# First queries and keys computed side by side as x arrives, the next weights loaded ahead of the other query and key weights, and the last store issued from ScalarE's queue

## The chip, the cores and the metric

The kernel runs on one core of a Trainium2 chip. The metric is the device time of one execution in microseconds (us). The profile names the engines PE (TensorE, the matmuls), PEld (TensorE's weight loads), DVE (VectorE), ACT (ScalarE), POOL (GpSimd) and SP (SyncE, which issues most DMAs). SPq and ACTq are the instruction queues of SP and ScalarE, where their DMAs are issued.

## The reference

One layer of a decoder for 512 prompt tokens and 8 x 4 sample tokens (544 columns together, d_model 1024), all in fp32:

```
glu_a, glu_b, q, k, v, g_conv, g_att = split(x @ w_in)
u = glu_a * sigmoid(glu_b)
conv_out = silu(layer_norm(causal_depthwise_conv(u, 31 taps))) @ w_conv_proj
o = stick_breaking_attention(q, [past_k, k], [past_v, v])   # samples: 4096 past tokens by pages
mixed = (sigmoid(g_conv)*conv_out + sigmoid(g_att)*(o @ w_att_proj)) @ w_out
x = layer_norm(2**0.25 * x + mixed)
x = layer_norm(2**0.25 * x + (silu(gate) * up) @ w_ffn_down + sigmoid(x @ w_ple_gate) * (p @ w_ple))
```

The past keys and values of the samples are 256 pages each, found by a page table. The outputs are the new x, k, v and the last GLU rows.

## The kernel before, in words

**Products.** Everything lies transposed, channels on the partitions and the 544 tokens in the columns. An fp32 matrix is split into a high part (fp32r) and a low part (the rest); a product of one 128 x 128 weight tile with one x chunk is three passes, high x high, high x low and low x high (`passes`, `products`). `products(p, cols, nk, rhs, base, ks)` adds up `nk` chunks in one PSUM tile; `gemm` takes a PSUM tile `g` (2 x 512 columns, two buffers) and does all eight. For queries and keys only the 512 prompt columns are computed this way (`PROMPT`).

**Weights.** `W` is a row of units of 128 x 1024 fp32 (512 KB, eight 128 x 128 tiles) in the order of use. `ORDER` begins with units q0, k0, b0, a0, v0 (units 0 to 4), then q1, k1 and so on; b and a are the two halves of the GLU. `w_load` issues a unit's load from SP, `w_split` splits one half of it (512 columns) with `split`: the high part goes to ScalarE (or VectorE), the low part, wl, to VectorE or GpSimd. Split halves live in four buffers each (`wh`, `wl`). `FIRST` is the list of the eight query and key units, 0, 1, 5, 6, 10, 11, 15 and 16. They lie in slots of their own (`wq`); other units come through three buffers `wr`.

**Sample projection.** The samples' 32 columns are projected apart: `first_sample` waits for all of x, and then `project` multiplies x, not split, with all eight query and key units (z<-wq,xr, 128 matmuls), in two halves: the queries' four units, then the keys'. Its result goes through two transposes to `qblk` and `ks`, and `decode` begins. `scores` and `decode` run over K/V pages, which `prefetch` loads from SP into at most 17 slots `kv`; the slots come free when the scores and the weighted sums are done.

**Order.** The program is written out by a planner, `Weave`. `main` is a generator that writes the large matmuls; side streams (loads, splits, prompt attention, convolution, decode) have a priority and are stepped whenever their condition holds by the planner's own clocks: `wv.t` for TensorE, `act`, `dve`, `pool`, and `dma` with 0.357 MB a microsecond. `wv.ready` keeps for each tile, by name, the time at which it is ready by those clocks. So the order of each engine's instructions is fixed when the program is built, and a change in the first instructions can shift the order of all that follow. On the chip the engines then wait for one another by semaphores.

**The start.** `main` writes ten warming matmuls, then issues from SP the eight x chunks (272 KB each), with the two halves of unit 0 behind x chunks 0 and 1 (the first half from ScalarE's queue), then the constants `cvt`, `cct` and the page table `ptt`. The other seven units of `FIRST` follow. The side stream `start` splits each x chunk at the time at which the planner expects it; after chunk 1 it starts `loader` (units 2, 3, 4 into `wr`, and later ones as buffers come free) and `splitter` (unit 1 on). The queries of unit 0 and the keys of unit 1 are two gemms, one after the other, each evacuated by ScalarE into `qk`.

**The end.** The last norm's second half is finished by `last`: four tiles of two chunks each; VectorE multiplies, ScalarE applies gain and bias (for chunk 7, VectorE does), and SP stores the output rows: chunks 0, 1, 6 and 7 each by its own DMA, the others in pairs (`give`).

Of the kernel before, what the change touches and what calls it, by code (L numbers as in the profile page):

```python
# [12 lines left out]
AF = mybir.ActivationFunctionType  # L13
# [7 lines left out]
NT = 544  # L21
HT = 272
# [11 lines left out]
BASE, NU = {}, 0  # L34
# [141 lines left out]
def step_kernel(ctx: ExitStack, tc: tile.TileContext, xT, pT, ck, cvv, state, pt, W, cv, cc, yT, kT, vT, cvo):  # L176
    nc = tc.nc
# [21 lines left out]
    def slot(name, shape=(128, 2, NT), dt=F32):  # L199
        return big.tile(list(shape), dt, tag="s", bufs=NSLOT, name=name)  # L200
# [26 lines left out]
    def load(eng, out, in_):  # L227
        eng.dma_start(out=out, in_=in_)  # L228
        moved(out)
        wv.ready[out.name] = wv.dma + 1.5  # L230
# [140 lines left out]

    def loader():
        for u in range(NU):
            if u in FIRST:
                continue
            if u in AGAIN:
                yield lambda: AGAIN[u] in kept
                raw[u] = kept.pop(AGAIN[u])
                continue
            if u in SLOTTED:  # L380
                yield lambda: u * 8 <= cur["pos"] + 8 * WAHEAD
            elif u in PAIR and u == PAIRS[PAIR[u]][1]:
                yield lambda: u * 8 <= cur["pos"] + 40 and cur["wp"] < 3
            else:
                yield lambda: u * 8 <= cur["pos"] + 32 and cur["raw"] < 3
            w_load(u)

    def splitter():
        for u in range(1, NU):
            if u in PAIR:  # L390
                if u == min(PAIRS[PAIR[u]]):
                    yield lambda: u * 8 <= cur["pos"] + 15
                    yield from pair_splits(PAIR[u])
                continue
            yield lambda: u in raw and u * 8 <= cur["pos"] + 15
            yield on(raw[u])
            for e in range(2):
                if held(u) == "w":
                    yield lambda: cur["w"] < 4
                w_split(u, e)  # L400
# [229 lines left out]
    qk = []  # L630
# [438 lines left out]
    def first_sample(xr, wq):  # L1069
        yield on(*xr)  # L1070
        o = []
        yield from project(8, lambda k: xr[k // 2][:, k % 2, 512:544],
                           lambda c, k: wq[ORDER.index(("qk"[c // 4], c % 4))][:, k * 128:(k + 1) * 128], o)
        xr.clear()
        wq.clear()
        tp = o.pop()
        for m in range(4):
            for hh in range(2):
                r = slice(64 * hh, 64 * hh + 64)
                V.tensor_scalar(out=qblk[r, :, m, (2 * m + hh) * 4:(2 * m + hh) * 4 + 4],  # L1080
                                in0=tp[r, m * 32:(m + 1) * 32].rearrange("p (s q) -> p s q", q=4),
                                scalar1=0.125, scalar2=None, op0=ALU.mult)
        V.tensor_copy(out=ks.rearrange("p m q -> p (m q)"), in_=tp[:, 128:256])
        flag.add("qs")
        wv.add(decode(), 1)
# [18 lines left out]
    def main():  # L1104
# [4 lines left out]
            T.matmul(warm[:, :128], lhsT=on_m, rhs=on_m, start=True, stop=True)  # L1109
        del warm  # L1110
        xr = [slot("xr") for g in range(4)]
        raw[0] = slot("wq", (128, 1024))
        come = {}
        for c in range(8):
            load(nc.sync, xr[c // 2][:, c % 2], xT[c // 2][:, c % 2 * NT:(c % 2 + 1) * NT])
            come[c] = wv.dma + 1.5
            if c < 2:
                h = slice(512 * c, 512 * c + 512)
                load(nc.scalar if c == 0 else nc.sync, raw[0][:, h], W[0][:, h])
                come["w", c] = wv.dma + 1.5  # L1120
            if c == 7:
                load(nc.sync, cvt, cv)
                load(nc.sync, cct, cc)
                load(nc.sync, ptt, pt)
        for u in FIRST[1:]:
            w_load(u)
        nc.gpsimd.memset(qblk, 0.0)
        nc.gpsimd.memset(anew, 0.0)
        nc.gpsimd.memset(eps, EPS)
        wv.add(first_sample(list(xr), dict(raw)), 2)  # L1130
        wv.add(prefetch(), 0)
        wv.add(sample_tail(), 4)
        x_tiles.extend((slot("xh", dt=F32R), slot("xl", dt=F32R)) for g in range(4))

        def start():
            for c in range(8):
                yield At(come[c])
                h, lo = (t[:, c % 2] for t in x_tiles[c // 2])
                x_hl.append((h, lo))
                split(h, lo, xr[c // 2][:, c % 2])  # L1140
                if c < 2:
                    yield At(come["w", c])
                    w_split(0, c)
                if c == 1:
                    wv.add(loader(), -1)
                    wv.add(splitter(), -1)
            xr.clear()
        wv.add(start(), -1)

# [16 lines left out]
        vs = v2 = None  # L1166
        wv.add(prompt_attention(), 2)
        wv.add(conv(), 3)
        for w, m in ORDER:
            o = []  # L1170
            if w in "qk":
                yield from gemm(xin, 8, o, PROMPT)
            else:
                yield from gemm(xin, 8, o)
            p = o.pop()
            if w == "q":
                qk.append(slot("qk"))
                S.activation(out=qk[m][:, 0, 0:512], in_=p[:, 0], func=AF.Copy, scale=0.125)
            elif w == "k":
                S.activation(out=qk[m][:, 1, 0:512], in_=p[:, 0], func=AF.Copy)  # L1180
                flag.add(("k", m))

                def keys(m=m, t=qk[m]):
                    yield done("qs")
                    V.tensor_copy(out=t[:, 1, 512:544], in_=ks[:, m])
                    yield on(t)
                    store(kT[m], t[:, 1])
                wv.add(keys(), 0)
            elif w == "b":
                u = slot("u", (128, 814))  # L1190
                us[m] = u
                nc.gpsimd.memset(u[:, 0:30], 0.0)
                load(nc.sync, u[:, 542:814], state[m])
                yield spare(2)
                sg = tmp("sg")
                sigmoid(sg, p[:, :, :HT], sg, halves(sg), ("sg", m))
            elif w == "a":
                wv.add(glu(m, us[m], p, sg), 0)
                sg = None
            else:  # L1200
                yield spare(1)
                vt = tmp("vt")
                S.activation(out=halves(vt), in_=p[:, :, :HT], func=AF.Copy)
                wv.when(on(vt), lambda m=m, vt=vt: store(vT[m], vt))
                if m % 2 == 0:
                    v2 = slot("v", (128, 2, 512))
                if m == 0:
                    vs = slot("vs", (128, 2, 512))

                def back(m=m, vt=vt, v2=v2):  # L1210
                    yield wv.bank("tp")
                    tp = bank("tp")
                    for kt in range(4):
                        tr(tp[:, kt * 128:(kt + 1) * 128], vt[:, kt * 128:kt * 128 + 128])
                    V.tensor_copy(out=v2[:, m % 2], in_=tp)
                    v_sb[m] = v2[:, m % 2]

                    def sample():
                        yield wv.bank("tp")
                        tp = bank("tp")  # L1220
                        for r in range(2):
                            tr(tp[:, r * 128:(r + 1) * 128], vt[:, 400 + 16 * r:528 + 16 * r])
                        V.tensor_copy(out=vs[:, :, m * 128:(m + 1) * 128],
                                      in_=tp[:, :256].rearrange("p (r c) -> p r c", r=2))
                        drop()
                        if m == 3:
                            v_sb["vs", 0], v_sb["vs", 1] = vs[:, 0], vs[:, 1]
                    wv.when(on(v2), sample)
                wv.when(on(vt), back)
# [389 lines left out]
        def last(i, p):  # L1619
# [41 lines left out]
            for g in range(4):  # L1661
                if g > 1:
                    centred(g)
                V.tensor_tensor(out=xs[g], in0=xs[g], in1=r.to_broadcast([128, 2, HT]), op=ALU.mult)
                yield on(xs[g])
                for i in range(2 * g, 2 * g + 2):
                    if i == 7:
                        V.tensor_scalar(out=xs[g][:, 1], in0=xs[g][:, 1], scalar1=cvt[:, L2G + i:L2G + i + 1],
                                        scalar2=cvt[:, L2B + i:L2B + i + 1], op0=ALU.mult, op1=ALU.add)
                    else:  # L1670
                        S.activation(out=xs[g][:, i % 2], in_=xs[g][:, i % 2], func=AF.Identity,
                                     scale=cvt[:, L2G + i:L2G + i + 1], bias=cvt[:, L2B + i:L2B + i + 1])
                    if g in (0, 3):
                        nc.sync.dma_start(out=yT[i][:, HT:], in_=xs[g][:, i % 2])
                if g in (1, 2):
                    give(g, HT)

# [130 lines left out]
```

## Time and profile before

| | |
|---|---|
| time of three runs | 993.13 us median, 991.53 to 996.7 |
| time of the profiled execution | 992.45 us |
| span of its profile, first to last instruction | 990.6 us |
| mean granted TensorE clock | 0.986 |
| busy: PE, PEld, DVE, ACT, POOL | 950.3, 831.2, 781.3, 539.2, 163.2 us |
| moved by DMA | 222 MB, 224 GB/s over the span |

The time of an execution holds 1.85 us more than the span. In the page's 40 slices a digit is the busy share of a slice of 24.8 us in tenths. In the timeline each row is: start, duration, engine, line, operation, output<-inputs, shape and count, and in brackets the idle time of the engine before it and what ended that. Line L146 stands for all operations of VectorE, ScalarE and GpSimd (they go through one helper), L238 for all matmuls, L228 for all loads, L1674 and L1578 for stores of the output.

### The profile page before, as it was taken

The page shows a single profiled execution, that of the slowest core. Times are in us where ns is not written, and L with a number is a line of the kernel's source. Part 1 is how long each engine was busy: PE and PEld are TensorE (multiplying, and loading weights), DVE is VectorE, ACT ScalarE, POOL GpSimd, SP SyncE. Part 2 cuts the span into 40 slices and gives each one's busy share as a digit, 9 for nine tenths or more (in the row PEclk, how much of TensorE's full clock was granted, in tenths as well). Part 3 has the DMA queues.
Part 4 walks back from the last instruction along what each step waited for, and adds up shares of the span by engine and source line. Part 5 has one row for each costly group of instructions (what it writes and reads, how often), then busy time and mean ns, then how long its engine had stood idle before and what let it go on. Part 6 is the DMA issues. An engine that isn't in the chain of part 4 may idle for free.

```text
span 990.6 us, 22509 instructions
## 1 busy us (share of the span) xinstructions
PE 950.3 (96%) x8026; PEld 831.2 (84%) x8026; DVE 781.3 (79%) x1288; ACT 539.2 (54%) x1042; POOL 163.2 (16%) x147
## 2 busy tenths in 40 slices
PE   9989999999899999999999889999999999999995
PEld 7866566667677887788878789999999999999994
DVE  3798798999964666466698687999999999943366
ACT  4634766575786785244467564544554555622224
POOL 1230313223211102033343110000000000220020
PEclk9999899999999999999999899999999999999998
DMA  9948989999989999999999635223223221322302
GB/s 356 339 160 298 336 301 330 313 324 328 311 281 339 311 346 330 342 367 351 325 335 352 250 108 193 86 88 126 86 91 123 86 95 56 100 93 87 128 1 90
DMA packets 101393, 222.00 MB, mean 224 GB/s; under 512 B 11169, under 2 KB 14498, under 8 KB 101282
## 3 DMA queue, kind: packets, MB, share of 16 engines
q1 hardware_dynamic: 99410, 217.46, 62.5%
q10 hardware_dynamic: 1872, 3.11, 0.8%
q8 instruction: 63, 1.03, 0.4%
q14 instruction: 48, 0.39, 0.1%
HBM read 215.45 MB, written 5.07 MB: 223 GB/s over the span
## 4 chain that ended last, share of the span: by engine, by line
PE 74%; DVE 10%; DMA 9%; SPq 3%; issue 2%; ACT 2%; POOL 0%; ACTq 0%; DVEq 0%; POOLq 0%
PE g L238 44%; PE z L238 10%; PE av L238 9%; PE o L238 5%; PE tp L238 5%; DVE c L146 3%; DMA kv<-in_cvv 2%; SPq L228 2%; DMA kv<-in_ck 2%; DVE pb L146 2%; DMA wr<-in_W 2%; PE tp L243 1%; DMA xr<-in_xT 1%; SPq L657 1%; DMA wa<-in_W 1%
## 5 line engine op out<-in xcount | busy, mean ns | idle before, releaser
L146 ACT ACTIVATE wh<-wr 128x512 fp32r<-128x512 f32 x236 | 146.9, 628 | 201.1 <-PE g L238 99.8
L146 DVE TENSOR_TENSOR wl<-wr,wh 128x512 fp32r<-128x512 f32 x196 | 135.1, 694 | 52.1 <-ACT wh L146 50.8
L146 POOL TENSOR_TENSOR wl<-wr,wh 128x512 fp32r<-128x512 f32 x44 | 70.2, 1598 | 493.0 <-DVE pw L146 259.8
L238 PE MATMUL g<-xh,wh 128*128 128x272 f32 (+1 forms) x512 | 127.6, 320 | 0.3 <-ACT wh L146 0.3
L238 PE MATMUL g<-h,wh 128*128 128x272 f32 x704 | 122.2, 290 | 0.0
L238 PE MATMUL g<-xl,wh 128*128 128x272 f32 (+1 forms) x512 | 119.3, 304 | 0.8 <-DVE xl L146 0.8
L238 PE MATMUL g<-xh,wl 128*128 128x272 f32 (+1 forms) x512 | 118.8, 303 | 0.2 <-POOL wl L146 0.2
L146 DVE SCALAR_TENSOR_TENSOR c<-u,cvt,c 128x512 f32<-128x512 f32 x120 | 111.6, 930 | 3.3
L238 PEld LDWEIGHTS g<-h,wh 128*128 128x128 f32 x704 | 103.2, 189 | 0.3
L238 PEld LDWEIGHTS g<-xh,wh 128*128 128x128 f32 x512 | 82.9, 191 | 22.2 <-issue 17.5
L238 PEld LDWEIGHTS g<-xl,wh 128*128 128x128 f32 x512 | 83.7, 191 | 3.6 <-DVE xl L146 1.5
L238 PEld LDWEIGHTS g<-xh,wl 128*128 128x128 f32 x512 | 83.1, 191 | 4.0 <-POOL wl L146 0.9
L238 PE MATMUL g<-h,wl 128*128 128x272 f32 x352 | 80.1, 289 | 0.0
L146 ACT ACTIVATE wh<-wq 128x512 fp32r<-128x512 f32 x87 | 54.5, 628 | 40.5 <-PE g L238 29.5
L238 PE MATMUL z<-kv,qblk 128*32 128x256 f32 x1024 | 64.6, 381 | 1.1 <-DMA kv<-in_ck 1.1
L238 PE MATMUL g<-x1h,wh 128*128 128x272 f32 (+2 forms) x216 | 64.0, 296 | 0.0
L238 PE MATMUL av<-kv,dp 128*32 128x512 f32 x512 | 63.8, 612 | 0.0
L146 DVE TENSOR_TENSOR wl<-wq,wh 128x512 fp32r<-128x512 f32 x75 | 54.6, 733 | 11.4 <-ACT wh L146 11.0
L238 PE MATMUL g<-x1l,wh 128*128 128x272 f32 (+2 forms) x216 | 62.6, 290 | 0.0
L238 PE MATMUL g<-x1h,wl 128*128 128x272 f32 (+2 forms) x216 | 62.6, 290 | 0.0
L146 ACT ACTIVATE pa<-pa 128x384 f32<-128x384 f32 (+1 forms) x96 | 52.5, 555 | 17.2 <-DVE pa L146 15.6
L238 PEld LDWEIGHTS g<-h,wl 128*128 128x128 f32 x352 | 58.0, 188 | 0.0
(315 smaller groups left out, 2352.8 us busy)
## 6 DMA issues: line engine op xcount, KB each, us to landing
kv<-in_ck SPq DMA_DIRECT2D x256, 256.0 KB, 4.4
kv<-in_cvv SPq DMA_DIRECT2D x256, 256.0 KB, 5.4
wr<-in_W SPq DMA_DIRECT2D x98, 512.0 KB, 4.2
wq<-in_W SPq DMA_DIRECT2D x37, 512.0 KB, 5.1
wa<-in_W SPq DMA_DIRECT2D x12, 512.0 KB, 10.2
xr<-in_xT SPq DMA_DIRECT2D x8, 272.0 KB, 5.6
out_yT<-pw SPq DMA_DIRECT2D x6, 272.0 KB, 2.3
out_kT<-qk ACTq DMA_DIRECT2D x4, 272.0 KB, 6.1
```

The costliest lines, as they stand in the source:

```text
L146: fn(**kw)
L228: eng.dma_start(out=out, in_=in_)
L238: T.matmul(out, lhsT=lhsT, rhs=rhs, start=start, stop=stop)
L243: T.transpose(out, in_, ident)
L657: reg[col] = nc.sync.value_load(ptt[0:1, col:col + 1], min_val=0, max_val=POOL - 1)
```

## The change

- Both units 0 and 1 get their slots at once, and the first loads go in one list: x chunk 0, first half of unit 0, x 1, x 2, first half of unit 1, x 3, second half of unit 0, x 4, x 5, second half of unit 1, x 6, x 7. `start` splits them in this order.
- Behind the constants, units 2 and 3 are loaded ahead of the other six units of `FIRST`. `loader` begins with unit 4, `splitter` with unit 2, and both are started after the last x chunk is split.
- The first queries and the first keys share one PSUM tile (columns of its two halves). Their products alternate: query chunk k, then key chunk k - 2. Both are evacuated behind the last key product.
- The store of chunk 7 at the end is issued from ScalarE's queue.

```
-            if u in FIRST:                                   # loader
+            if u in FIRST or u < 4:
-        for u in range(1, NU):                               # splitter
+        for u in range(2, NU):
...
-        raw[0] = slot("wq", (128, 1024))
+        for u in range(2):
+            raw[u] = slot("wq", (128, 1024))
         come = {}
+        first = (0, ("w", 0, 0), 1, 2, ("w", 1, 0), 3, ("w", 0, 1), 4, 5, ("w", 1, 1), 6, 7)
+        for i, c in enumerate(first):
+            if c in range(8):
+                load(nc.sync, xr[c // 2][:, c % 2], xT[c // 2][:, c % 2 * NT:(c % 2 + 1) * NT])
+            else:
+                h = slice(512 * c[2], 512 * c[2] + 512)
+                load(nc.scalar if i == 1 else nc.sync, raw[c[1]][:, h], W[c[1]][:, h])
             come[c] = wv.dma + 1.5
...
-        for u in FIRST[1:]:
+        for u in (2, 3, *FIRST[2:]):
             w_load(u)
...
         def start():
+            for c in first:
                 yield At(come[c])
+                if c in range(8):
+                    h, lo = (t[:, c % 2] for t in x_tiles[c // 2])
+                    x_hl.append((h, lo))
+                    split(h, lo, xr[c // 2][:, c % 2])
+                else:
+                    w_split(*c[1:])
+            wv.add(loader(), -1)
+            wv.add(splitter(), -1)
...
+        for u_, (w, m) in enumerate(ORDER):
             o = []
+            if u_ == 0:
+                base = cur["next"]
+                cur["next"] += 16
+                p = gps()
+                for k in range(10):
+                    for i, kk in ((0, k), (1, k - 2)):
+                        if 0 <= kk < 8:
+                            yield from products(p, [(i, 0, 512)], 8, xin, base + 8 * i, ks=(kk,))
+            elif u_ > 1:
...
-                S.activation(out=qk[m][:, 1, 0:512], in_=p[:, 0], func=AF.Copy)
+                S.activation(out=qk[m][:, 1, 0:512], in_=p[:, int(u_ == 1)], func=AF.Copy)
...
-                        nc.sync.dma_start(out=yT[i][:, HT:], in_=xs[g][:, i % 2])
+                        (nc.scalar if i == 7 else nc.sync).dma_start(out=yT[i][:, HT:], in_=xs[g][:, i % 2])
```

More of the change, by code (lines that the diff above doesn't have):

```diff
@@ L1111, in main @@
         xr = [slot("xr") for g in range(4)]
-        raw[0] = slot("wq", (128, 1024))
+        for u in range(2):
+            raw[u] = slot("wq", (128, 1024))
         come = {}
-        for c in range(8):
-            load(nc.sync, xr[c // 2][:, c % 2], xT[c // 2][:, c % 2 * NT:(c % 2 + 1) * NT])
-            come[c] = wv.dma + 1.5
[L1117 to L1124, printed above, removed]
-        for u in FIRST[1:]:
+        first = (0, ("w", 0, 0), 1, 2, ("w", 1, 0), 3, ("w", 0, 1), 4, 5, ("w", 1, 1), 6, 7)
[5 more added lines that the diff above has]
+                load(nc.scalar if i == 1 else nc.sync, raw[c[1]][:, h], W[c[1]][:, h])
+            come[c] = wv.dma + 1.5
+        load(nc.sync, cvt, cv)
+        load(nc.sync, cct, cc)
+        load(nc.sync, ptt, pt)
+        for u in (2, 3, *FIRST[2:]):
             w_load(u)
@@ L1129, in main @@
         nc.gpsimd.memset(eps, EPS)
-        wv.add(first_sample(list(xr), dict(raw)), 2)
+        wv.add(first_sample(list(xr), {u: raw[u] for u in FIRST}), 2)
         wv.add(prefetch(), 0)
@@ L1135, in start @@
         def start():
-            for c in range(8):
+            for c in first:
                 yield At(come[c])
[L1138 to L1146, printed above, removed]
+                if c in range(8):
[6 more added lines that the diff above has]
+            wv.add(splitter(), -1)
             xr.clear()
@@ L1168, in main @@
         wv.add(conv(), 3)
-        for w, m in ORDER:
+        for u_, (w, m) in enumerate(ORDER):
             o = []
[L1171 to L1175, printed above, removed]
+            if u_ == 0:
[7 more added lines that the diff above has]
+            elif u_ > 1:
+                if w in "qk":
+                    yield from gemm(xin, 8, o, PROMPT)
+                else:
+                    yield from gemm(xin, 8, o)
+                p = o.pop()
             if w == "q":
```

## The prediction

> **What bounds the kernel now.** I read the page first (span, slices, chain), then the windows, then the timeline of the first 30 us and of the end, then the waits.
>
> ```profile
> span 990.6 us, 22509 instructions
> PE   9989999999899999999999889999999999999995
> DMA  9948989999989999999999635223223221322302
> PE 74%; DVE 10%; DMA 9%; SPq 3%; issue 2%; ACT 2%; POOL 0%; ACTq 0%; DVEq 0%; POOLq 0%
> 0.00:25.00 25.00, 22.73 (x208) 18.04 (x209) 10.11 (x15) 12.13 (x19) 4.58 (x10) 1.00 0.94 356
> 50.00:75.00 25.00, 20.57 (x162) 15.94 (x160) 24.23 (x34) 9.05 (x20) 7.78 (x6) 0.93 0.44 160
> 75.00:575.00 500.00, 481.82 (x4283) 376.43 (x4280) 385.41 (x627) 310.55 (x635) 118.82 (x109) 0.98 0.92 321
> 575.00:975.00 400.00, 396.81 (x3129) 395.97 (x3129) 334.80 (x557) 183.31 (x317) 24.61 (x13) 1.00 0.27 94
> ```
>
> Columns of the last four rows: length, busy PE, PEld, DVE, ACT, POOL, granted clock, DMA share, GB/s. TensorE sets the time: 481.82 of 500 us, then 396.81 of 400. So a microsecond that TensorE saves at the start reaches the end, unless the K/V stream (DMA share 0.92 for 500 us) paces the middle: only then is the start worth nothing. The change touches the first 30 us and the last store. There the rows are these (start, duration, engine, line, operation):
>
> ```profile
> 5.97 0.80 PE L238 MATMUL g<-xh,wh 128*128 128x512 f32 x1 [0.33 <-ACT wh L146]
> 9.66 0.50 PE L238 MATMUL g<-xl,wh 128*128 128x512 f32 x1 [0.78 <-DVE xl L146]
> 16.06 0.39 PE L238 MATMUL g<-xh,wl 128*128 128x512 f32 x1
> 16.29 0.40 PE L238 MATMUL g<-xh,wh 128*128 128x512 f32 x1
> 19.86 3.70 PE L238 MATMUL z<-wq,xr 128*32 128x128 f32 x128
> 23.49 0.52 PE L238 MATMUL g<-xh,wh 128*128 128x272 f32 x2
> 26.08 0.41 PE L238 MATMUL g<-xh,wh 128*128 128x272 f32 x2
> 26.83 0.41 PE L238 MATMUL g<-xh,wh 128*128 128x272 f32 x2
> 5.50 5.60 DMA xr<-in_xT
> 13.15 1.15 ACT L146 ACTIVATE wh<-wq 128x512 fp32r<-128x512 f32 x2 [1.38 <-DMA wq<-in_W]
> 22.17 2.43 ACT L146 ACTIVATE wh<-wr 128x512 fp32r<-128x512 f32 x4 [1.61 <-DMA wr<-in_W]
> 13.84:19.86 6.02, 6.02 (x26) 4.35 (x25) 1.27 (x2) 0.95 (x2) 0.00 (x0) 1.00 1.03 413
> ```
>
> The reader is to see that full matmuls follow each other by 0.23 us (16.06 to 16.29), so a product (three passes of one k) is 0.70 us for queries or keys and 0.75 us for the gate unit (26.08 to 26.83). Queries and keys need 48 x 0.232 = 11.1 us and took 19.86 - 5.97 = 13.9: 2.8 us of waiting, for x (row 9.66 and its like) and for the key weights, which landed at 13.15. Then the sample projection (z<-wq,xr, 3.63 us to 23.49), then unit 2, the "b" half of the GLU, whose weights landed at 22.17.
>
> **The change part by part.**
>
> *Order of loads.* The bytes are the same; the order is new. At 413 GB/s a 512 KB unit takes 1.3 us, half of one 0.65. The last x chunk landed at 5.50 + 5.60 = 11.1; two key halves now stand ahead of it: 12.4. Units 2 and 3 now stand ahead of the six other query and key units: unit 2 lands at 13.15 + 1.3 = 14.5 instead of 22.17. In return those six come 2.6 us later. Unit 2 was right behind them, so the last key unit landed near 20.9 and the last query unit near 19.6: now 23.5 and 22.2. SP issues the same number of descriptors ahead of the first K/V page, so the stream starts where it did.
>
> *The interleaved row.* The first product still starts at 5.97: x chunk 0 and the first half come first, as before. With two products to each chunk, TensorE's 1.4 us cover one chunk and half of a weight half (0.7 + 0.65/2 to 0.65 us). What can still hold it is the splitting into high and low parts:
>
> ```profile
> 5.43 0.73 DVE L146 TENSOR_TENSOR xl<-xr,xh 128x544 fp32r<-128x544 f32 x1 [5.43 <-ACT xh L146]
> 6.50 1.38 DVE L146 TENSOR_TENSOR xl<-xr,xh 128x544 fp32r<-128x544 f32 x1 [0.34 <-ACT xh L146]
> 8.25 4.54 DVE L146 TENSOR_TENSOR xl<-xr,xh 128x544 fp32r<-128x544 f32 x6 [0.37 <-ACT xh L146]
> 6.00 3.03 POOL L146 TENSOR_TENSOR wl<-wq,wh 128x512 fp32r<-128x512 f32 x2 [3.87 <-ACT wh L146]
> 7.56 4.22 ACT L146 ACTIVATE xh<-xr 128x544 fp32r<-128x544 f32 x6 [0.30 <-DMA xr<-in_xT]
> ```
>
> Low parts of x take 0.73 us alone and 1.38 beside a low part of a weight half on POOL (1.5 each). The code sends a low part to POOL when its own clock has VectorE behind, and with x chunks queued there I expect all four halves on POOL. VectorE then has 8 x 0.73 and some 4 x 0.65 of delay from 5.43 on: 13.9, and with small gaps 14.4 for the last x. Behind it stand the last two passes of that product and three key products: 0.46 + 2.1, and TensorE's own backlog (q7, k5, k6, k7 after it had been held in the first four) brings the end of the row to 18.2. Bounds: 17.1 (5.97 + 11.1, no wait at all) and 19.2 (below). So the row ends 1.7 us sooner, 0.6 to 2.8. The query evacuation now comes after the keys, 0.6 us on ScalarE twice, in a bank that the next unit doesn't need.
>
> The Trainium skill, page "SBUF — State Buffer", section "SBUF: two separate sides", speaks against this step: it says that VectorE with two SBUF inputs and GpSimd hold one port pair by an exclusive lock for a whole instruction, so that the loser stops. By that rule four POOL operations of 1.5 us would come on top of 8 x 0.64 (the page's full block): 5.43 + 11.1 = 16.6 for the last low part, and 19.2 for the row's end. The 1.38 us row bears contention out, at 0.65 of a POOL operation rather than all of it.
>
> *The sample projection's place.* It stood behind the keys; now unit 2 is ready first. Its place is fixed when the program is written: by the planner's clock (an order, not a time on the chip), which keeps one time of readiness for a tile, the first weight half counts as ready only with its second, and its row ends late (about 21); the projection's query weights count as ready at 23.3, which is four unit-2 products of 0.69 later. On the chip four products end at 18.2 + 4 x 0.75 = 21.2, and TensorE then stands until the last query unit lands, 22.2: a new wait of 1.0 us that takes the place of the old ones. It ends at 22.2 + 3.6 = 25.8. Before, the same work (projection and four products) was done at 23.49 + 3.0 = 26.5. Gain of these parts together: 0.7 us. Since the projection waits for its landing, the row's end (17.1 or 19.2) hardly changes this. The place does: with six or more products ahead it is 1.7, with three 0, with none 25.8 - 23.49 = 2.3 us lost.
>
> *Splits of units 2 and 3.* ScalarE does them from 14.5 on, when it has nothing else; buffers of halves come free with q3 and k3. Hidden behind the row, which runs to 18.2; if the row ended before them, a half would cost its 0.6 us.
>
> *What comes later because of it.* The sample's queries feed the decode stream, whose first scores free K/V buffers:
>
> ```profile
> 25.58 1.60 DVE L146 TENSOR_SCALAR qblk<-tp 64x32 f32<-64x32 f32 x8
> 50.78 22.62 SPq L228 DMA_DIRECT2D kv<-in_ck  x8
> SPq L228 <- PE z L238: 13.4, 1, 13.4
> 65.06 1.93 PE L238 MATMUL z<-kv,qblk 128*32 128x256 f32 x32
> 58.09 0.55 PE L243 MATMUL tp<-cct,vt 128*128 128x128 f32 x2 [4.43 <-DVE v L146]
> PE z L238 <- DMA kv<-in_ck: 1.1, 3, 0.6
> ```
>
> The projection ends 25.8 - 23.49 = 2.3 us later. SP stood 13.4 us for the first scores at 65.06, with the DMA share at 0.44; if the chain from qblk to there is tight, the hole grows by up to 2.3. The hardest row for the price is the last one: in the whole run TensorE waited 1.1 us for pages of keys. I take 0 and keep 2.3 for the range. The 4.43 us wait at 58.09 is VectorE behind with convolution and attention, and the new order may mend or double it: -4.4 to +4.4, taken as 0, since nothing in the change moves work off VectorE there.
>
> *The last store.*
>
> ```profile
> 986.59 0.61 ACT L146 ACTIVATE pw<-pw,cvt 128x272 f32<-128x272 f32 x1 [0.28 <-DVE pw L146]
> 986.59 0.42 DVE L146 TENSOR_SCALAR pw<-pw,cvt 128x272 f32<-128x272 f32 x1
> 987.23 0.84 SPq L1674 DMA_DIRECT2D out_yT<-pw  x2
> 30.31 0.35 ACTq L233 DMA_DIRECT2D out_kT<-qk  x1
> ```
>
> SP issues stores 6 and 7 one behind the other, 0.42 each, after ScalarE's 987.20. Store 7 needs only VectorE's 987.01. On ScalarE's queue it is issued from 987.23 on, beside store 6: 0.4 us sooner (0 if the two then share the engines badly). ScalarE has nothing queued behind it. The Trainium skill, page "DMA: Bandwidth & Descriptors", section "Issuing engines are not separate DMA queues", says that a second issuing engine saves only the issue time; by that rule the gain is the same 0.42 and no more.
>
> Sum: -0.7 - 0.4 = -1.1 us. The profiled execution took 992.45 (span 990.6), so 991.35; the middle of the three runs shown, 993.13, is 0.7 above it. I say 991.3. Changes under 0.5% (5 us) can't be told from none.
>
> **The rivals.**
>
> *The new order helps later, faster.* If decode, attention and convolution fall so that VectorE isn't behind at 58, the 4.43 us wait goes too: 991.35 - 4.4 = 986.9. For it: VectorE is busy 24.23 of 25 us there, and unit 2's GLU comes sooner, which spreads its work. Against: the same work has to pass VectorE by then.
>
> *The K/V stream sets the time, slower.* The hole in the DMA ends with the first scores; if these move by 2.3 us and the stream paces everything to 575 us, TensorE's gain is void: 992.45 + 2.3 - 0.4 = 994.4. For it: share 0.92 for 500 us and 13.4 us of SP's wait. Against: TensorE's 1.1 us. It decides from the point at which the first scores start after 65.06 and the stream's end moves with them; from 5.4 us on (a projection put behind unit 3's products too: 18.2 + 16 x 0.75 + 3.6 = 33.8, 10.3 late) it is over 0.5%, up to 1002.
>
> *The front doesn't gain.* By the lock (row's end 19.2) with three products ahead of the projection the start gives 0, and the store alone stays: 992.0.
>
> **How the numbers follow.** My forecast 0.55; helped later 0.18; stream 0.13 under 0.5% and 0.08 over; no gain at the front 0.06. Faster is the second (986.9 is 0.56% under): 0.18. Slower is the 0.08. The rest, 0.74, is the same. The range runs from 986.5 to 995.5: it takes in the 986.9 and the 994.4 with the spread of the runs about them, and leaves out the far slow end. The forecast's own range is 989.5 to 993, by the bounds of the place.
>
> **What would show it.** Right: the first row of products ends near 18.2 with q and k passes alternating; unit 2 starts at once behind it; z<-wq,xr starts near 22.2 after a wait of about 1 us for wq's DMA, with about four unit-2 products ahead of it; wl on POOL four times; the last store's row on ScalarE's queue at 987.2 of the old clock. Wrong: first scores later than 65 and SP's wait above 13.4 us, or the wait for v at 58 gone or doubled; a projection ahead of unit 2.

## The result and the profile after

The changed kernel took 1018.34 us in the median of four executions (1015.27 to 1020.55); the kernel before, on the same chip, 992.8 us (991.53 to 996.7). The ratio is 1.0252, with a 95% interval of 1.0228 to 1.0277: slower by 25 us, against a forecast of 991.3 with a range up to 995.5.

The profiled execution took 1017.47 us. Its page begins so (TensorE's busy time, then its tenths and the DMA share's in 40 slices):

```profile
span 1015.7 us, 22545 instructions
PE 958.4 (94%) x8026; PEld 831.0 (82%) x8026; DVE 783.9 (77%) x1282; ACT 539.4 (53%) x1039; POOL 176.3 (17%) x156
PE   8978989989979999999998799999999999999995
DMA  9929879999989999999998815232232321332302
```

The number of matmuls is the same, 8026. The span is 25.1 us longer. TensorE is busy 958.4 us instead of 950.3, +8.1; the rest of the span, in which it stands, is 1015.7 - 958.4 = 57.3 us instead of 990.6 - 950.3 = 40.3, +17.0. So about two thirds of the loss is waiting and one third is matmuls at a lower granted clock (mean 0.978 instead of 0.986): busy time times granted clock is 937 us in both, 950.3 x 0.986 and 958.4 x 0.978.

Where the waiting lies is read from windows (length, busy PE, PEld, DVE, ACT, POOL, granted clock, DMA share, GB/s). First the kernel before:

```profile
75.00:175.00 100.00, 93.06 (x784) 64.95 (x781) 87.42 (x147) 60.29 (x124) 23.59 (x25) 0.97 0.92 315
175.00:300.00 125.00, 118.06 (x1038) 90.45 (x1040) 111.35 (x176) 86.96 (x176) 30.63 (x27) 0.99 0.91 311
300.00:500.00 200.00, 199.33 (x1723) 160.25 (x1715) 125.04 (x192) 113.22 (x225) 42.62 (x40) 1.00 0.96 340
500.00:625.00 125.00, 118.19 (x1106) 107.15 (x1105) 104.28 (x193) 78.81 (x164) 24.67 (x19) 0.97 0.65 233
```

The same windows of the changed kernel:

```profile
0.00:25.00 25.00, 22.16 (x110) 17.87 (x114) 12.65 (x13) 11.80 (x18) 7.71 (x13) 0.86 0.94 348
75.00:175.00 100.00, 90.31 (x743) 63.47 (x740) 83.38 (x142) 59.25 (x123) 21.60 (x24) 0.95 0.87 290
175.00:300.00 125.00, 113.28 (x962) 83.60 (x962) 107.90 (x169) 78.64 (x160) 35.90 (x32) 0.97 0.89 302
300.00:500.00 200.00, 199.12 (x1724) 157.99 (x1727) 124.38 (x194) 117.47 (x227) 32.85 (x35) 1.00 0.96 335
500.00:625.00 125.00, 110.49 (x1049) 93.12 (x1041) 94.28 (x168) 73.15 (x157) 39.92 (x29) 0.96 0.70 248
```

The reader sees that most of the 25 us doesn't lie where the change is. In the first 25 us TensorE is busy 22.16 us, before 22.73, but part of this is matmuls at half clock (0.86 in the first window). By the work done, the start is 2 us behind: the projection and three unit-2 products are done at 28.03 (row below), in the kernel before at 26.08. Between 75 and 300 us TensorE's busy time is 2.8 + 4.8 us short, and between 500 and 625 us 7.7: together 15.2. From 300 to 500 the two agree, though the share of the DMA is highest there. From 75 to 300 prompt attention and decode are both woven in between the large matmuls (in the kernel before ScalarE writes prompt attention's tile pa from 31 to 307 us, and TensorE multiplies pages from 65 to 544). From 500 to 625 decode ends and the first FFN products (g<-x1h) begin, at 536.4 instead of 519.2 us.

The start itself (start, duration, engine, line, operation):

```profile
6.20 0.50 PE L238 MATMUL g<-xh,wh 128*128 128x512 f32 x1 [0.92 <-ACT wh L146]
7.58 0.50 PE L238 MATMUL g<-xh,wl 128*128 128x512 f32 x1 [0.64 <-POOL wl L146]
6.30 1.52 DVE L146 CAST xh<-xr 128x544 fp32r<-128x544 f32 x1
7.86 7.80 DVE L146 TENSOR_TENSOR xl<-xr,xh 128x544 fp32r<-128x544 f32 x7
14.61 0.63 ACT L146 ACTIVATE wh<-wr 128x512 fp32r<-128x512 f32 x1 [1.48 <-DMA wr<-in_W]
22.06 0.41 PE L238 MATMUL g<-xh,wh 128*128 128x272 f32 x2
24.39 3.70 PE L238 MATMUL z<-wq,xr 128*32 128x128 f32 x128
28.03 0.52 PE L238 MATMUL g<-xh,wh 128*128 128x272 f32 x2
29.30 1.61 DVE L146 TENSOR_SCALAR qblk<-tp 64x32 f32<-64x32 f32 x8 [5.87 <-PE tp L243]
63.21 0.69 PE L243 MATMUL tp<-cct,vt 128*128 128x128 f32 x2 [5.25 <-DVE v L146]
70.15 1.93 PE L238 MATMUL z<-kv,qblk 128*32 128x256 f32 x32
```

Its windows there, and of the waits of SP's queue the one for the first scores (total, times, longest):

```profile
6.00:9.00 3.00, 1.95 (x5) 1.10 (x6) 2.97 (x4) 2.20 (x5) 2.14 (x2) 0.87 1.01 372
9.00:12.00 3.00, 2.93 (x7) 1.82 (x7) 3.00 (x3) 2.73 (x5) 2.74 (x3) 0.50 1.05 390
12.00:15.00 3.00, 3.00 (x9) 2.32 (x8) 3.00 (x5) 1.44 (x3) 1.24 (x2) 0.50 1.06 411
```

```profile
SPq L228 <- PE z L238: 21.5, 5, 20.2
```

The row of products ends at 22.06 instead of the 18.2 forecast. The granted clock is 0.50 from 9 to 15 us. The projection comes behind three unit-2 products, with no wait, and the first scores start at 70.15 instead of 65.06; SP stands 20.2 us for them instead of 13.4.

TensorE's list of matmuls, compared by tiles and shapes with that of the kernel before, has 689 in another place. The program issues 6897 matmuls; the profile counts 8026, since some leave two records, as the ten warming ones do. The order of the row itself doesn't count in this, since its tiles bear the same names.

### The profile page after: what moved, and what is told of

Read it like the earlier page. It is cut to its first block, busy times and chain, and to the rows that moved or that the text cites. A ratio compares the mean times of both kernels' runs of the same rounds, so it can differ in the third digit from the quotient of the medians.

```text
span 1015.7 us, 22545 instructions
## 1 busy us (share of the span) xinstructions
PE 958.4 (94%) x8026; PEld 831.0 (82%) x8026; DVE 783.9 (77%) x1282; ACT 539.4 (53%) x1039; POOL 176.3 (17%) x156
## 4 chain that ended last, share of the span: by engine, by line
PE 67%; DMA 3%; DVE 3%; ACT 2%; issue 2%; SPq 1%; POOL 1%; POOLq 0%; DVEq 0%; ACTq 0%
PE g L238 40%; PE z L238 9%; PE av L238 8%; PE o L238 5%; PE tp L238 4%; DMA kv<-in_cvv 1%; DMA wr<-in_W 1%; SPq L228 1%; POOL wl L146 1%; PE tp L243 1%; DMA kv<-in_ck 1%; DVE pw L146 1%; ACT pa L146 0%; SPq L657 0%; ACT ga L146 0%
## 5 line engine op out<-in xcount | busy, mean ns | idle before, releaser
L146 ACT ACTIVATE wh<-wr 128x512 fp32r<-128x512 f32 x232 | 144.8, 629 | 214.2 <-PE g L238 108.8
L146 POOL TENSOR_TENSOR wl<-wr,wh 128x512 fp32r<-128x512 f32 x50 | 82.4, 1655 | 541.5 <-ACT wh L146 271.6
L146 DVE TENSOR_TENSOR wl<-wr,wh 128x512 fp32r<-128x512 f32 x190 | 131.5, 696 | 54.0 <-ACT wh L146 48.0
```

The costliest lines, as they stand in the source:

```text
L146: fn(**kw)
```

## The experiments

Four explanations stood against each other. *Clock*: the half clock at the start costs time and delays all that follows. *Late projection*: the sample projection 4.5 us later makes the K/V stream late. *Loads or row*: one part of the change is itself the cost. *Order*: the planner's clock differs after the first 20 us, so it writes another program, in which the engines fit worse. All ratios are to the kernel before, timed beside it on the same chip. e1, e2, e3 and e9 were executed twice each, e7 and e8 eight times, e5, e6, e10 and e11 ten times.

**e1, warm clock.** The changed kernel with 14 warming matmuls instead of ten; all else is in the same order.

```
-        for i in range(10):
+        for i in range(14):
```

> The changed kernel with 14 warming matmuls in place of 10, so that TensorE is busy until 6.1 instead of 5.3 us; every other instruction and its order are those of the changed kernel. Theory 'clock' (the half clock from 8.2 to 15.0 us and the late sample projection behind it cost the 25 us, grown by the K/V stream): the clock stays whole, the first row of products ends near 19 instead of 22.2, z<-wq,xr starts near 22.5, the first scores come near 67, and most of the 25 us is gone: 993 to 1000. Theory 'order' (the order of the instructions behind the start, which the planner wrote anew, costs it): the row ends near 19 as well, but the time falls by 0 to 4 us only: 1014 to 1018.

1017.75 us, ratio 1.0263 (1.023 to 1.0297). The window of e1 that answers to the last one above:

```profile
12.00:15.00 3.00, 2.88 (x11) 2.09 (x12) 3.00 (x5) 1.45 (x3) 1.22 (x2) 1.00 1.03 406
```

The clock stays at 1.00, the row ends at 20.59, 1.5 us sooner, and the first scores start at 69.45, 0.7 sooner. The time does not follow. The clock at the start is not the cause of the 25 us.

**e2, units 2 and 3 behind the other six.** The changed kernel, with the one load order put back.

```
-        for u in (2, 3, *FIRST[2:]):
+        for u in (*FIRST[2:], 2, 3):
```

> The changed kernel with units 2 and 3 loaded behind the other six query and key units, as before the change; the interleaved row and the store on ScalarE's queue stay. The planner then puts the sample projection directly behind the row again. Theory 'late projection' (units 2 and 3 ahead delay the samples' queries by 3.7 us, and the K/V stream with them): the first scores come at 65 us or sooner and the time is 990 to 996. Theory 'order': the planner writes a third order, whose time is not tied to the place of the projection; anything from 985 to 1025, and if it is over 1000 the late projection isn't the cause.

1005.6 us, ratio 1.0141 (1.0106 to 1.0176).

```profile
19.26 3.89 PE L238 MATMUL z<-wq,xr 128*32 128x128 f32 x128
49.70 1.93 PE L238 MATMUL z<-kv,qblk 128*32 128x256 f32 x32
```

The projection starts at 19.26, sooner than before (19.86), and the first scores at 49.70, 15 us sooner. Yet it is 14 us slower than before, and 790 matmuls stand elsewhere. An early projection and an early K/V stream do not save it: "late projection" can't be the whole, and the projection's place cannot be read as a lever by itself.

**e3, only units 2 and 3 ahead.** The kernel before, with no interleaved row and the old last store.

```
-            if u in FIRST:
+            if u in FIRST or u < 4:
...
-        for u in FIRST[1:]:
+        for u in (1, 2, 3, *FIRST[2:]):
```

> The kernel before, with units 2 and 3 loaded ahead of the other six query and key units, and nothing else of the change: queries and keys one after the other, all stores from SP. Theory 'late projection': the projection stands behind unit 2's first products and ends 2 to 4 us later than before, and the time is 1010 to 1020, as with the whole change. Theory 'clock': no half clock at the start, so 993 to 998. Theory 'order': again an order of its own, 985 to 1025.

1018.5 us, ratio 1.0271 (1.0221 to 1.0321), like the whole change. In TensorE's list 734 of the 6897 matmuls stand elsewhere than before. Either this load order is the cost by itself, or it too leads the planner to a poor order. e6, e10 and e11 tell these apart.

**e5, the change in the old order.** The loads of the first two units, the splits and the interleaved row are written by hand as in the changed kernel (the row in two PSUM tiles), and the last store is on ScalarE's queue. Units 2 and 3 stay behind. The planner runs over the old start without writing it, so its clocks and the order of everything behind the row are those of before.

```
+        first = (0, ("w", 0, 0), 1, 2, ("w", 1, 0), 3, ("w", 0, 1), 4, 5, ("w", 1, 1), 6, 7)
...
+        wv.dry = u < 2          # clock counted, instruction not written
...
+        for k in range(10):
+            for i, kk in ((0, k), (1, k - 2)):
...
+                    T.matmul(row[i][:, 0], lhsT=wh, rhs=xh, start=kk == 0, stop=False)
...
-                        nc.sync.dma_start(out=yT[i][:, HT:], in_=xs[g][:, i % 2])
+                        (nc.scalar if i == 7 else nc.sync).dma_start(out=yT[i][:, HT:], in_=xs[g][:, i % 2])
```

> The interleaved loads, splits and row of the changed kernel and its last store, with units 2 and 3 behind the other six, and with every instruction behind the row in the order of the kernel before: the planner runs on the clocks of the kernel before. Theory 'order': 990 to 993 if TensorE's clock stays whole in the first 15 us (row ends near 18.5, 1 us sooner than before), 993 to 995 if it halves there as in the changed kernel. Theory 'clock': if the clock halves at the start, 1005 or more. Theory 'late projection': 989 to 993.

992.01 us in ten executions, ratio 0.9991 (0.9969 to 1.0013).

```profile
19.11 0.40 PE L1185 MATMUL g<-xh,wl 128*128 128x512 f32 x1
19.44 1.79 PE L242 MATMUL z<-wq,xr 128*32 128x128 f32 x50
```

With the old order kept, the row ends and the projection starts 0.4 us sooner than before (19.44, 19.86), and the time is about 1 us lower, which can't be told from none. That is the size the forecast gave to the start and the store.

**e6, the same with units 2 and 3 physically ahead.** The order of the engines is that of e5; only the two loads are issued first.

```
+        for u in (2, 3):
+            early[u] = big.tile([128, 1024], F32, tag="wr", bufs=3, name="wr")
+            nc.sync.dma_start(out=early[u], in_=W[u])
```

> As the kernel with the interleaved row and the old order behind it, and now units 2 and 3 are loaded ahead of the other six query and key units as well. The projection stays directly behind the row, so TensorE waits there for the last key unit: z<-wq,xr ends near 25 instead of 23.4. Theory 'late projection': this delay grows through the K/V stream and costs most of the 25 us, 1005 or more. Theory 'order': it costs what is seen at the start and no more, 992 to 995.

997.03 us in ten executions, ratio 1.0038 (1.0014 to 1.0062): 5 us more than e5.

```profile
22.33 5.35 PE L242 MATMUL z<-wq,xr 128*32 128x128 f32 x122 [2.15 <-DMA wq<-in_W]
69.35 1.93 PE L242 MATMUL z<-kv,qblk 128*32 128x256 f32 x32
```

In an order that expects the query weights first, TensorE stands 2.15 us for them, the clock falls to half, and the first scores come at 69.35, 4.8 us later than in e5 (64.59). So the load order costs 5 us in this order, not 25. That is more than the theory "order" expected (992 to 995), and far less than "late projection" did (1005 or more). First scores as late as the changed kernel's (70.15) go with 997 us.

**e7, e8, e9, the planner's clock set on.** The kernel before, with no instruction added or taken out; the planner's clock of TensorE is set on by 0.4, 0.6 or 3.0 us behind the first keys, once.

```
             p = o.pop()
+            wv.t += 0.6 * (w == "k" and m == 0)      # e8; 0.4 in e7, 3.0 in e9
```

> The kernel before, with the planner's TensorE clock set 0.4 us on behind the first keys; no instruction is added, removed or changed, only the order that the planner writes may differ. Here it stays nearly that of the kernel before. All theories: 990 to 996.

> The same with 0.6 us: again the same instructions, and the planner writes another order from about 25 us on. Theory 'order': 1000 to 1020, since the order alone sets the time. Theories 'clock' and 'late projection': loads, the row and the projection are those of the kernel before, so 990 to 996.

> The same with 3.0 us, about what the planner's clock was late behind the row in the changed kernel. Theory 'order': 1000 to 1020 and not the time of the 0.6 us kernel. Theories 'clock' and 'late projection': 990 to 996.

| clock set on by | us | ratio | TensorE's matmuls in another place | first scores |
|---|---|---|---|---|
| 0.4 us (e7) | 992.91 | 1.0006 (0.9989 to 1.0023) | 0 | 65.5 |
| 0.6 us (e8) | 1000.47 | 1.0085 (1.0068 to 1.0103) | 824 | 48.7 |
| 3.0 us (e9) | 1010.79 | 1.0187 (1.016 to 1.0214) | 797 | 49.0 |

In e7 no engine's list differs from that of the kernel before. In e8 and e9 nothing is added to the chip's work either, but the planner, which also chooses the engine of a split by its clocks, hands a few operations to another engine: the pages count 1288, 1042 and 147 operations on VectorE, ScalarE and GpSimd before, 1296, 1038 and 143 in e8, and 1286, 1041 and 150 in e9, 2477 each time. The rewritten order, with these few moves, costs up to 18 us. Between 0.4 and 0.6 the program tips over into another: the first scores come sixteen us earlier, and the sample's last projections (z<-wa) fall in front of the first FFN products (g<-x1h). (The profiled execution of e8, 995.03 us, is the fastest of its eight; the others took 999.67 to 1002.61.) In e9:

```profile
537.24 1.96 PE L238 MATMUL z<-wa,o_s 128*32 128x128 f32 x64 [0.55 <-DVE o_s L146]
546.20 0.38 PE L238 MATMUL g<-x1h,wh 128*128 128x256 f32 x1
```

In the kernel before z<-wa is woven in behind the start of g<-x1h, and nothing stands in front of that (operations of one tile: count, shortest, median and longest ns, first and last start):

```profile
L238 PE MATMUL g<-x1h,wh x216: 276/291/582, 519.2 to 834.0; 128*128 128x272 f32 x44, 128*128 128x256 f32 x32, 128*128 128x288 f32 x32
```

```profile
L238 PE MATMUL z<-wa,o_s x64: 420/421/421, 550.8 to 554.0; 128*32 128x128 f32 x64
```

The changed kernel is slow in another way: there z<-wa comes at 581.0, behind the start of g<-x1h (536.4) as in the kernel before, and g<-x1h itself starts late.

**e10, e11, the whole change in another order.** The changed kernel as it was timed, with the planner's clock set on by 0.2 or 0.7 us at the same place.

```
                 p = o.pop()
+            wv.t += 0.7 * (w == "k" and m == 0)      # e11; 0.2 in e10
```

> The whole change as it was timed, its instructions, loads and first rows untouched; only the planner's clock is set on by 0.2 us behind the first keys, so that the later program is written in another order. Theory 'order' (most of the 25 us is one bad order that the planner wrote from a clock the change had moved): another order need not be as bad; start and store are worth about -1 us and the late projection about +5 (e6 against e5), so with an order as good as that of before it takes 995 to 1002 us, ratio 1.002 to 1.009, and the first rows are those of the changed kernel (row's end 22, first scores near 70). Rival 'the change's own start' (late row, projection after the row, units 2 and 3 ahead, half clock at 8 to 15 us carry the 25 us by themselves): 1014 to 1020 us again, ratio 1.022 to 1.028, since all of them stay.

> The whole change again, the planner's clock set on by 0.7 us in place of 0.2. Theory 'order': a third order of the same instructions, which lands anywhere between 995 and 1015 us, as the two clocks set on by 0.6 and 3.0 us in the kernel before did (ratio 1.002 to 1.022), and differs from the run with 0.2 us by more than the measurement's 0.3%, or agrees with it if the two orders are nearly the same. Rival 'the change's own start': 1014 to 1020 us, like the changed kernel and like the run with 0.2 us.

e10: 994.79 us, ratio 1.0023 (0.9996 to 1.0049). e11: 994.0 us, ratio 0.9999 (0.9972 to 1.0027). Both in ten executions. In both, only 12 of TensorE's matmuls stand elsewhere than in the kernel before, where the changed kernel has 689: the passes of the two unit-2 products that now stand ahead of the projection. The shift of the clock has led the planner back to the old program behind the new start. TensorE's list is the same in e10 and e11, so they are two timings of one order and not two orders. Both came out slightly under what was expected (995 to 1002, and 995 to 1015). The start of e11:

```profile
21.45 0.41 PE L238 MATMUL g<-xh,wh 128*128 128x272 f32 x2
23.04 3.70 PE L238 MATMUL z<-wq,xr 128*32 128x128 f32 x128
67.58 1.93 PE L238 MATMUL z<-kv,qblk 128*32 128x256 f32 x32
```

Its windows:

```profile
12.00:15.00 3.00, 3.00 (x11) 2.37 (x10) 3.00 (x4) 1.45 (x3) 1.09 (x1) 0.69 1.04 408
75.00:175.00 100.00, 94.67 (x799) 66.63 (x797) 87.39 (x143) 58.85 (x121) 24.73 (x26) 0.97 0.94 314
175.00:300.00 125.00, 118.01 (x1013) 90.11 (x1009) 112.14 (x177) 85.40 (x174) 30.60 (x27) 0.97 0.91 310
500.00:625.00 125.00, 118.36 (x1106) 105.62 (x1105) 103.50 (x191) 77.58 (x162) 25.40 (x20) 0.97 0.67 244
```

This decides it. All parts of the change are there: units 2 and 3 ahead, the row, which ends at 21.45, the clock below full speed, the projection behind two unit-2 products and 3 us later than before, the store. Yet the time is that of before. The three windows hold 4.4, 4.7 and 7.9 us more of TensorE's work than in the changed kernel: 17.0 us. The spans differ by 1015.7 - 994.4 = 21.3, and 958.4 - 954.9 = 3.5 of them is longer busy time for the same number of matmuls (mean granted clock 0.978 and 0.981). What TensorE waited for in the changed kernel between 75 and 300 us (total, times, longest), and in e11 in the same window:

```profile
PE tp L243 <- ACT pa L146: 7.2, 4, 3.3
PE tp L243 <- ACT dp L146: 4.9, 2, 3.8
PE z L238 <- ACT pa L146: 3.2, 1, 3.2
PE tp L243 <- DVE v L146: 2.7, 2, 2.4
PE z L238 <- DMA kv<-in_ck: 2.1, 2, 1.7
PE tp L243 <- DMA kv<-in_cvv: 1.3, 1, 1.3
```

```profile
PE tp L243 <- ACT pa L146: 7.3, 4, 2.5
...
PE tp L238 <- ACT dp L146: 1.1, 1, 1.1
```

The wait for prompt attention's pa is the same in both, 7.2 and 7.3. New in the changed kernel are 4.9 + 3.2 us in which TensorE reaches a transpose of decode and a product before ScalarE has done its step; e11 has 1.1 of them. Also new are 2.1 + 1.3 us in which TensorE waits for pages (kv); e11 has no such wait there. These don't carry the loss: e1, with the changed kernel's order and time, waits 0.3 us for pages in its whole run, and e10, which takes the time of before, 3.1 us in its whole run.

## Why the prediction was wrong

**The step that failed is "-4.4 to +4.4, taken as 0": the price of the rewritten order.** The prediction knew that the order is fixed by the planner's clock and that the first instructions can shift all that follow. Then it bounded the price by one wait, the 4.43 us for v at 58, as if the new program could differ only there. That wait grew by 0.8 us, to 5.25; the rest of the loss arose between 75 and 300 us and between 500 and 625. A bound from one row of the old order says nothing of an order not yet seen. The runs give the real width: by their medians, programs with none or 12 of TensorE's matmuls in another place take 992 to 997 us (e5, e6, e7, e10, e11), those with 689 to 824 take 1000 to 1019 (after, e2, e3, e8, e9); and one and the same change takes 994.0 and 994.79 in one order and 1018.34 us in the other.

**The sum of the parts, -1.1 us, was neither borne out nor refuted, and its first term had the wrong sign.** With the old order, and units 2 and 3 left behind, e5 gives about -1 (0.9991, interval from -3 to +1 us); all parts in nearly the old order, e10 and e11, give +2.3 and -0.1 us by their ratios. None can be told from zero. The start was to gain 0.7 us. By the work done it is 2 us behind in the changed kernel (28.03 to 26.08), and in e10 and e11, where the third unit-2 product starts at 26.22 and 26.67 instead of 25.24, 1.0 and 1.4. So where e11 ends level, that is not the gain that was forecast.

**The row's end, 18.2 (bounds 17.1 and 19.2): wrong, 22.06.** Two things were missing. The planner gave the high part of one x chunk to VectorE (1.52 us), so the last low part ended at 15.66 instead of 14.4. And TensorE's clock fell to half. In e10, whose first rows are those of the changed kernel, the row ends at 19.95, with matmuls of 0.39 or 0.40 us from 9.98 on where the changed kernel's take 0.63 until 14.37; in e1 it ends at 20.59, and with the splits placed by hand (e5) at 19.34 (19.11 + 0.23). All three are above the upper bound.

The four POOL low parts came as foreseen (rows 6.23, 8.16 and 11.71 of the timeline: 1.30, two in 3.29, and 1.47). The first ran beside VectorE's cast. Beside each of the other three one low part of x took 1.80 us on VectorE (starts 8.51, 10.23 and 11.96), the other five 0.71 to 0.73: three delays of 1.07, together 3.2 us, where the sum had four of 0.65, 2.6. The 0.65 was misread: the row of 1.38 in the kernel before began at 6.50, half a microsecond into a POOL operation (6.00 to 7.30), and lost only the rest of it. It ended at 7.88, 0.58 after that operation. The three here end at 10.31, 12.03 and 13.76, and the POOL operations beside them at 9.73, 11.45 and 13.18: 0.58 later each time.

The Trainium skill, page "SBUF — State Buffer", section "SBUF: two separate sides", by whose exclusive lock the loser stops until the other instruction has ended, agrees with these ends. The prediction set this rule against its own 0.65, and the rule fits better. But the prediction's 19.2 added POOL's durations whole, and they hold waits of their own: 1.47 to 1.76 for these three, where the shortest of this kind in the trace takes 1.26.

**Unit 2 lands at 14.5: right** (the wait for it ended at 14.61). **Four products ahead of the projection and a wait of 1.0 us: three and none**. The planner's clock put three there; the wait was gone because the row was late. In e10 the wait shows, 0.65 us. **The projection 2.3 us later: 4.5** (24.39 to 19.86 at its start). Its price "0, at most 2.3" was too small for an order made for early weights (5 us, e6), and near right where two unit-2 products stand ahead of it (e10, e11).

**The rivals.** "The K/V stream sets the time" foresaw the right signs, first scores later (70.15) and SP's wait above 13.4 us (20.2), and by its own rule 5.1 us late is at most 0.5%. In e6 scores 4.3 us late go with +0.4%, as that rival said. But e11 has them 2.5 us late at no cost, and e2, e8 and e9 have them 15 us early and are slower. "The new order helps later" had the right lever and the wrong sign. "The front doesn't gain" (992.0, the store alone) fits what is left once the order is taken out: the start gained nothing in e10 and e11.

**The last store: -0.4 forecast, about -0.2 measured.**

```profile
1011.77 0.61 ACT L146 ACTIVATE pw<-pw,cvt 128x272 f32<-128x272 f32 x1 [0.28 <-DVE pw L146]
1012.22 0.34 ACTq L1683 DMA_DIRECT2D out_yT<-pw  x1
1012.41 0.34 SPq L1683 DMA_DIRECT2D out_yT<-pw  x1
```

The summary of line L1683, which issues the single stores:

```profile
DMA to landing us min/median/max: 1.8/1.9/2.1
```

From the start of ScalarE's last operation to the end of the span it is 3.88 us (1015.655 - 1011.77, by the trace's unrounded span); before, 4.06 (990.649 - 986.59). It is 3.88 or 3.89 in all seven traces with the store on ScalarE's queue and 4.05 to 4.07 in the five without: 0.18 saved. SP's last issue now begins right when ScalarE ends (1012.38), as foreseen. But the slowest of this line's stores now lands 2.1 us after its issue, where all took 1.8 before. The Trainium skill, page "DMA: Bandwidth & Descriptors", section "Issuing engines are not separate DMA queues", says that a second issuing engine saves only the issue time. That is 0.42 here, and the traces keep 0.18 of it.

**Left open.** Which single swap in the changed kernel's order costs most was not tried; the runs show that the order costs it, and the waits show where, not which decision of the planner comes first. The one order tried in which the whole change is not slower is the old one but for 12 matmuls. The clock's 8.1 us go with the waits, but no run separates the two.

## What to carry to other kernels

Where a planner writes a program's order, compare the instruction lists of the two kernels first: a change at the start that moves a tenth of a tuned list is a change of everything, and here each of the five such lists was slower, by 0.9 to 2.7%. To learn what the change itself is worth, hold the old order, or lead the planner back to it by a small shift of its clock; here that was 0.2 us. In a forecast, the price of a rewritten order is taken from what other orders of the same work cost, not from one wait of the old one, and here it was a loss each time.

## What the runs showed of the hardware

TensorE's granted clock fell to 0.50 in the changed kernel's start after waits of only 0.92 and 0.64 us (rows 6.20 and 7.58). In the windows shown above TensorE was busy 1.95 of 3 us from 6 to 9, and then seven and nine matmuls took 3 us each, where the kernel before did 13 from 12 to 15 us. The Trainium skill, page "TensorE: Matmul & The Clock Gate", section "Part 1: The HAM clock gate", speaks of a free-running window of 3.4 us and of half the clock after one idle window. Here TensorE was busy 1.85 of the 3.41 us before the fall (4.78 to 8.19), and the clock fell all the same.

Whether it falls is not settled by the program alone. e7 is the kernel before, instruction for instruction. In its profile waits of 0.91 and 0.64 us came at the start, and the granted clock was 0.84 from 6 to 9 and 0.59 from 9 to 12, where the kernel before stayed at 1.00 after waits of 0.33, 0.16 and 0.78 us. e10's first rows are the changed kernel's, and its clock shows no fall in the first 30 us. In e1 four more matmuls left no wait ahead of the first product, and the clock stayed at 1.00; from one profile it isn't shown that they held it. The same half clock followed a wait of 2.15 us in e6. What decides between these cases no run here shows.

Beside a GpSimd subtraction, VectorE's subtraction of the same kind ended 0.58 us after GpSimd's, each of the four times named above (ends at 7.88, 10.31, 12.03 and 13.76), and 0.57 to 0.59 us after it in the four such pairs of e5, whether it took 1.33 or 1.81 us in all.
